# Hybrid GLA and convolution block: the mix projections as seven-product units, with the recurrent branch moved to the convolution's output projection

## The chip, the cores and the metric

The kernel runs on one core of one Trainium2 chip. The metric is the device time of one execution in microseconds (us), here the median over runs. Five engines work side by side, each through its own list of instructions in a fixed order: PE (TensorE, matmuls, with PEld for its weight loads), DVE (VectorE), ACT (ScalarE), POOL (GpSimd) and SP (SyncE, which here only issues transfers). They wait for each other by semaphores. POOL and ACT issue some of the transfers too.

## What is computed

A block of 1024 tokens plus 16 meta tokens in front (L = 1040; LQ = 1026 are kept), width 1024, in fp32:

```python
u = rms_norm(h, norm_mix_g)                 # h: meta tokens, then x
q, k, v, r, a_lr, c_in, g_gla, g_conf = split(u @ w_in)
o = gla_chunked(q, k, v, log_a(a_lr))       # gated linear attention, 4 heads, chunks of 64
o = rms_norm(o per head) * silu(r)
gla = o @ w_gla_o
c = c_in[:, :1024] * sigmoid(c_in[:, 1024:])
y = causal_dwconv(c, 31 taps) + bias        # each channel by itself
conv = silu(layer_norm(y)) @ w_conf_o
h = h + (sigmoid(g_gla) * gla + sigmoid(g_conf) * conv) @ w_out
h = h + gated ConvFFN(rms_norm(h))          # w_up, 3-tap convolution, silu gate, w_down
out = rms_norm(h) without the meta tokens
```

## The kernel before, in words

Activations lie channel by channel: a tile holds 128 channels by up to 1040 tokens. An fp32 matmul is emulated: every operand is split into a high part (float32r) and the rest, and `mm3` (L178) issues three matmuls for each of the 8 tiles of the inner dimension: high times high (L187), low times high (L188), high times low weights (L189). A block of 128 output channels is therefore 24 matmuls for each group of columns.

The program runs through these stages: the norm of x and three blocks by column chunks (alpha, q and k of head 0); 54 plain projection blocks (`block`, 72 matmuls of 342 to 348 columns each) for q, k, v, r, the two halves of c and the two gates; the GLA output projection (576 matmuls of 342 columns); the convolution's output projection (768 of 258 or 252); the projection w_out; the FFN's up projection; w_down.

The up projection already uses a seven-product scheme: two blocks of 128 outputs that share their inputs are a unit. The weights of both (raw tiles r1 and r2) are quartered and combined by four sums on POOL (L792 to L795), and the products of the combined weights with combined halves of the activations need 7 products of 24 matmuls in place of the 8 that two plain blocks would take for the same columns. `unit_weights` (L786) makes the weights w1, w21, w34 and w2 of a unit, `unit_products` (L823) issues the products and adds them up, and for the first four units `unit_head` issues two products ahead.

Plain weights are split in `load_w` (L171): a raw load on SP's queue, two copies on ACT (L173 makes the negated raw, L174 the high part), and a transfer from DRAM on POOL's queue that adds the raw values onto the first (L175), which leaves the low part. Tiles come from pools: three raw weight tiles, three split pairs, 35 slots of activations. An instruction that writes a tile waits until the readers of the tile's last user are done.

Beside the projections two generators are fed piece by piece by `tick()`, which every column group of a block calls. `conv` (L365) is the 31-tap convolution of one channel tile, one DVE instruction per tap (L367, then L370 on the whole tile, each on the result of the last), at 2.2 pieces a tick; POOL adds its result to `ysum` (L377). `gla` (L390) is one head of the recurrent branch, at 1.35 pieces a tick: decay factors from POOL, ACT and DVE at several band widths (L442 to L446), small matmuls on them (L457, L476), then the states chunk by chunk (L537 to L549) and the norm (L566). `layer_norm` (L612) runs beside the last gates. q, k, v and c go from PSUM into SBUF slots and are read there. A scheduler writes each engine's order from these calls, their priorities and dependences.

## Time and profile before

| what | value |
|---|---|
| median of 2 runs | 1843.58 us (1843.4 to 1843.75) |
| the profiled execution | 1847.21 us |
| its span in the trace | 1845.4 us |
| mean granted TensorE clock | 0.983 |
| PE busy | 1776.2 us, 96% |
| DVE, ACT, POOL busy | 1156.4, 705.6, 444.8 us |

The chain that ended last consists of PE to 80% and of DVE to 13%. A stage is read by its stretch: the plain projections with GLA and convolution beside them run from 64 to about 824 us, the GLA output projection to 915, the convolution's to 1007, w_out to 1101, the up projection to 1571, w_down to the end. In a stretch where PE is busy all the time, the number of matmuls and the length of one set the time; where it is not, another engine or a transfer does.

### The profile page before, as it was taken

How to read it: one execution, taken by the hardware profiler on the slowest of the kernel's cores; microseconds unless marked ns; L12 is line 12 of the kernel's file. 1: busy time of each engine (PE TensorE's matmuls, PEld its weight loads, DVE VectorE, ACT ScalarE, POOL GpSimd, SP SyncE). 2: the span in 40 equal slices, each digit the busy share in tenths (PEclk: the TensorE clock that was granted, in tenths of full speed). 3: DMA queues.
4: the chain of work that ended last, by engine and by line, in shares of the span. 5: the costliest groups of instructions: out<-in, count | busy, mean ns of one | idle time of the engine just before them, and what ended most of it. 6: DMA issues, size and time to landing. Idle time of an engine off the chain costs nothing.

```text
span 1845.4 us, 28931 instructions
## 1 busy us (share of the span) xinstructions
PE 1776.2 (96%) x12210; PEld 1692.7 (92%) x12210; DVE 1156.4 (63%) x1350; ACT 705.6 (38%) x1050; POOL 444.8 (24%) x333
## 2 busy tenths in 40 slices
PE   4999999999999999999999997999999999899997
PEld 3999999999999999999999997999999999677886
DVE  5239976968878860733455369877667666733523
ACT  5325436426435743691222333222222223423321
POOL 2103223313413412200000256333333334200000
PEclk7999999999999999999999998999999999999999
DMA  6343335324334544453133441222221224634532
GB/s 211 79 92 87 65 80 125 70 71 114 69 80 103 121 124 120 153 192 137 35 137 129 164 132 35 100 73 77 86 79 69 87 86 151 207 116 154 158 119 66
DMA packets 63442, 200.93 MB, mean 109 GB/s; under 512 B 6864, under 2 KB 14160, under 8 KB 63312
## 3 DMA queue, kind: packets, MB, share of 16 engines
q1 hardware_dynamic: 51168, 159.03, 26.4%
q0 software_dynamic: 10368, 37.75, 10.2%
q10 hardware_dynamic: 1776, 2.30, 0.4%
q8 instruction: 96, 1.57, 0.4%
q14 instruction: 34, 0.28, 0.0%
HBM read 162.31 MB, written 36.74 MB: 108 GB/s over the span
## 4 chain that ended last, share of the span: by engine, by line
PE 80%; DVE 13%; DMA 2%; issue 2%; ACT 2%; POOL 1%; SPq 0%; DVEq 0%; ACTq 0%; POOLq 0%
PE mm L187 13%; PE mm L188 13%; PE mm L189 13%; PE prod L187 12%; PE prod L189 12%; PE prod L188 12%; DVE y L370 5%; DVE opl L228 1%; DVE wl L162 1%; PE g L476 1%; DVE E L445 1%; DMA x<-in_xT 1%; PE g L544 1%; PE g L537 1%; PE g L545 1%
## 5 line engine op out<-in xcount | busy, mean ns | idle before, releaser
L187 PE MATMUL mm<-uh,wh 128*128 128x342 f32 (+4 forms) x1344 | 445.7, 332 | 0.0
L188 PE MATMUL mm<-ul,wh 128*128 128x342 f32 (+4 forms) x1344 | 435.0, 324 | 0.0
L189 PE MATMUL mm<-uh,wl 128*128 128x342 f32 (+4 forms) x1344 | 433.0, 322 | 0.0
L188 PE MATMUL prod<-opl,wh 128*128 128x258 f32 x1232 | 349.7, 284 | 12.1 <-DVE opl L228 11.8
L187 PE MATMUL prod<-oph,wh 128*128 128x258 f32 x1232 | 350.1, 284 | 4.8 <-DVE t L832 4.8
L189 PE MATMUL prod<-oph,wl 128*128 128x258 f32 x1232 | 350.4, 284 | 0.0
L370 DVE SCALAR_TENSOR_TENSOR y<-c,pv,y 128x1026 f32<-128x1026 f32 x240 | 342.3, 1426 | 5.4
L161 ACT ACTIVATE wh<-wr 128x1024 fp32r<-128x1024 f32 (+2 forms) x152 | 147.7, 974 | 382.5 <-PE prod L188 175.2
L162 DVE TENSOR_TENSOR wl<-wr,wh 128x1024 fp32r<-128x1024 f32 (+2 forms) x134 | 159.0, 1189 | 175.6 <-ACT wh L161 174.3
L187 PEld LDWEIGHTS mm<-uh,wh 128*128 128x128 f32 x1344 | 255.7, 190 | 5.4 <-issue 3.7
L188 PEld LDWEIGHTS mm<-ul,wh 128*128 128x128 f32 x1344 | 255.5, 190 | 1.7 <-issue 0.6
L189 PEld LDWEIGHTS mm<-uh,wl 128*128 128x128 f32 x1344 | 255.6, 190 | 0.7 <-issue 0.6
L188 PEld LDWEIGHTS prod<-opl,wh 128*128 128x128 f32 x1232 | 234.4, 190 | 13.3 <-DVE opl L228 12.7
L187 PEld LDWEIGHTS prod<-oph,wh 128*128 128x128 f32 x1232 | 234.4, 190 | 5.8 <-issue 3.2
L189 PEld LDWEIGHTS prod<-oph,wl 128*128 128x128 f32 x1232 | 233.9, 190 | 0.0
L189 PE MATMUL mm<-oph,wl 128*128 128x512 f32 (+1 forms) x374 | 143.6, 384 | 3.2 <-DVE wl L162 3.2
L187 PE MATMUL mm<-oph,wh 128*128 128x512 f32 (+1 forms) x374 | 143.9, 385 | 2.1 <-ACT wh L161 1.3
L188 PE MATMUL mm<-opl,wh 128*128 128x512 f32 (+1 forms) x374 | 144.6, 387 | 0.6 <-DVE opl L228 0.6
L187 PE MATMUL prod<-sh,wh 128*128 128x342 f32 (+2 forms) x448 | 133.8, 299 | 0.5 <-ACT gate L656 0.5
L175 POOL DMA_DIRECT2D wl<-in_w_mix x50 | 44.0, 880 | 372.2 <-ACT wl L173 318.3
L189 PE MATMUL prod<-sh,wl 128*128 128x342 f32 (+2 forms) x448 | 133.4, 298 | 0.0
L188 PE MATMUL prod<-sl,wh 128*128 128x342 f32 (+2 forms) x448 | 133.4, 298 | 0.0
(239 smaller groups left out, 2852.4 us busy)
## 6 DMA issues: line engine op xcount, KB each, us to landing
wr<-in_w_mix SPq DMA_DIRECT2D x56, 512.0 KB, 3.9
wl<-in_w_mix POOLq DMA_DIRECT2D x50, 512.0 KB, 8.1
wr<-in_w_up SPq DMA_DIRECT2D x48, 512.0 KB, 3.3
wr<-in_w_o SPq DMA_DIRECT2D x32, 512.0 KB, 3.5
wr<-in_w_dn SPq DMA_DIRECT2D x32, 512.0 KB, 3.6
act_d<-fy SPq DMA_DIRECT2D x21, 512.0 KB, 2.6
ar<-act_d POOLq DMA_DIRECT2D x21, 512.0 KB, 6.6
wr<-in_w_dn SPq DMA_DIRECT2D x16, 384.0 KB, 3.2
```

The costliest lines, as they stand in the source:

```text
L161: pin(S.activation(hi, raw, AF.Copy))
L162: (eng or V).tensor_tensor(lo, raw, hi.bitcast(F32), op=ALU.subtract)
L175: nc.gpsimd.dma_start(lo, src, accum_op=ALU.add)
L187: PE.matmul(out, whi[:, wk], hi[:, c0:c1], start=first and k == 0, stop=False)
L188: PE.matmul(out, whi[:, wk], lo[:, c0:c1], start=False, stop=False)
L189: PE.matmul(out, wlo[:, wk], hi[:, c0:c1], start=False, stop=last and k == n - 1)
L228: (eng or V).tensor_tensor(lo, src, hi.bitcast(F32), op=ALU.subtract)
L370: V.scalar_tensor_tensor(y[:, :LQ], c[:, j : j + LQ], pcol("dw_w", i * CONV_K + j), y[:, :LQ], op0=ALU.mult, op1=ALU.add)
L445: V.tensor_tensor(Ev[:, :, 0:s], Ev[:, :, 0:s], kv[:, :, 0:s], op=ALU.mult)
L476: PE.matmul(pt[:, c * half : (c + 1) * half].rearrange("p (b t) -> p b t", t=s), lt[:, sl], right(rt[:, sl], s), start=True, stop=True)
L537: PE.matmul(kv_ps[:, :DVH], kdT[:, c * CH : (c + 1) * CH], vc(c), start=True, stop=True)
L544: PE.matmul(op[:, :DVH], qd[:, c * CH : (c + 1) * CH], sts[c], start=True, stop=False)
```

## The change

The 54 plain blocks become 27 units of seven products (168 matmuls of 260 columns each), in this order: 8 units of c alternating with 8 of gates, 3 of q and k (heads 1 to 3), 4 of v, 4 of r. `unit_products` takes a new form for all units but the first four, here and in the FFN: partial results stay in two PSUM banks (`chain`, `twin`) onto which further products accumulate, and ACT copies the intermediate sums. The results of every unit go to DRAM (`done`), and their readers load them again. The weights of the new units are made with `by_dma`: the low parts of w1, w34 and w2 come from adding transfers on POOL's queue, of w34 with the combined tile in SBUF as its source, and POOL itself subtracts for w21. There are four split pairs in place of three, 34 slots of 1040 columns in place of 35 of 1056, and x and u lie in pairs of channel tiles per half of 520 tokens.

The convolution runs beside the units (1.9 pieces per product), reading c back from DRAM, its sum `ysum` is added up by a transfer, and the layer norm is queued behind it. After all units, GLA runs (5.8 pieces a tick, a second head may start while the first is in its states) beside the convolution's output projection, which now precedes the GLA output projection. Cut to its core, the diff is:

```diff
     wraw = ctx.enter_context(tc.tile_pool(name="wraw", bufs=3))
-    wspl = ctx.enter_context(tc.tile_pool(name="wspl", bufs=3))
+    wspl = ctx.enter_context(tc.tile_pool(name="wspl", bufs=4))
...
+    def split_from(src, raw):
+        hi, lo = weight_pair(raw.shape[-1])
+        pin(S.activation(lo, raw, AF.Copy, scale=-1.0))
+        pin(S.activation(hi, raw, AF.Copy))
+        nc.gpsimd.dma_start(lo, src, accum_op=ALU.add)
+        return hi, lo
...
+    active = []
...
+        if q is gla_q:
+            if not active:
+                active.append(q.popleft())
+            done = next(active[0], None)
+            if done is None:
+                active.pop(0)
+            else:
+                active.append(active.pop(0))
+                if done == 2 and q:
+                    active.append(q.popleft())
...
+    def conv(i):
+        c = slot(nm="c")
+        nc.sync.dma_start(c[:, :L], c_d[i])
+        taps = [META] + [j for j in range(CONV_K) if j != META]
+        for j in taps:
+            o = max(META - j, 0)
+            src, dst, wcol = c[:, j + o - META : j - META + LQ], y[:, o:LQ], pcol("dw_w", i * CONV_K + j)
+            if j == META:
+                V.tensor_scalar(dst, src, wcol, pcol("dw_b", i), op0=ALU.mult, op1=ALU.add)
+            else:
+                V.scalar_tensor_tensor(dst, src, wcol, dst, op0=ALU.mult, op1=ALU.add)
             yield 1
...
+        nc.gpsimd.dma_start(ysum_d, y[:, :LQ], **({"accum_op": ALU.add} if i else {}))
...
+        sr = [reload(sr_d[2 * h + d], "sr") for d in range(2)]
+        yield 2
...
+            PO.tensor_tensor(og[:, :LQ], og[:, :LQ], sr[d][:, :LQ], op=ALU.mult)
+            nc.sync.dma_start(og_d[2 * h + d], og[:, :LQ])
...
+    def unit_weights(src1, src2, ahead, full, by_dma):
+        with tc.high_priority(offset=ahead):
+            r1, r2 = load_raw(src1), load_raw(src2)
+            w1 = None
+            if full:
+                w1 = split_from(src1, r1) if by_dma else split_w(r1)
+            a11, a12, a21, a22 = r1[:, :512], r1[:, 512:], r2[:, :512], r2[:, 512:]
+            s1, s2 = Pt[:, 512:], Pt[:, :512]
+            PO.tensor_tensor(s1, a21, a22, op=ALU.add)
+            PO.tensor_tensor(s2, s1, a11, op=ALU.subtract)
+            PO.tensor_tensor(a11, a11, a21, op=ALU.subtract)
+            PO.tensor_tensor(a12, a12, s2, op=ALU.subtract)
+            if by_dma:
+                w21 = split_w(Pt, PO)
+                w34 = split_from(r1, r1)
+                return w1, w21, w34, split_from(src2[:, 512:], a22)
+            if full:
+                w21, w34 = split_w(Pt), split_w(r1, PO)
+            else:
+                w34, w21 = split_w(r1), split_w(Pt)
+            return w1, w21, w34, split_w(a22)
+
+    def product(w, c0, op, h, onto=None, more=False):
+        pt = bank("prod") if onto is None else onto
+        whi, wlo = w
+        for q in range(2):
+            out = pt[:, q * 512 : q * 512 + h // 2]
+            for k in range(4):
+                hi, lo = op[k // 2]
+                a0 = (k % 2) * h + q * h // 2
+                wk = slice(c0 + k * P, c0 + (k + 1) * P)
+                for x, y, n in ((whi, hi, 0), (whi, lo, 1), (wlo, hi, 2)):
+                    PE.matmul(out, x[:, wk], y[:, a0 : a0 + h // 2], start=onto is None and k == n == 0,
+                              stop=k == 3 and n == 2, skip_group_check=more or onto is not None)
+        tick()
+        return pt
+    def unit_head(w1, ops, h):
+        sums, halves = unit_parts(h)
+        a = slot(nm="fa")
+        p1 = halves(a[:, h:])
+        S.activation(p1, sums(product(w1, 0, ops["B11"], h)), AF.Copy)
+        V.tensor_tensor(halves(a), sums(product(w1, 512, ops["B21"], h)), p1, op=ALU.add)
+        return p1, a
...
+        chain = product(w1, 0, ops["B11"], h, more=True)
+        S.activation(a1, sums(chain), AF.Copy)
+        V.tensor_tensor(a0, sums(product(w1, 512, ops["B21"], h)), a1, op=ALU.add)
+        product(w21, 0, ops[2], h, chain, more=True)
+        S.activation(a1, sums(chain), AF.Copy)
+        twin = product(w21, 512, ops[1], h, more=True)
+        S.activation(b1, sums(twin), AF.Copy)
+        product(w34, 0, ops[3], h, chain)
+        S.activation(b0, sums(chain), AF.Copy)
+        V.tensor_tensor(b1, b1, b0, op=ALU.add)
+        product(w34, 512, ops["B22"], h, twin)
+        V.tensor_tensor(a1, sums(twin), a1, op=ALU.add)
...
+    C, GATE, QK, VAL, R = range(5)
+    units = [u for i in range(8) for u in ((C, i, NB_C2 + i, NB_C1 + i), (GATE, i, NB_G + i, NB_H + i))]
+    units += [(QK, h, NB_Q + h, NB_K + h) for h in range(1, HEADS)]
+    units += [(VAL, h, NB_V + 2 * h, NB_V + 2 * h + 1) for h in range(HEADS)]
+    units += [(R, h, NB_R + 2 * h, NB_R + 2 * h + 1) for h in range(HEADS)]
...
+            S.activation(a[:, :L], a[:, :L], AF.Sigmoid)
+            V.tensor_tensor(b[:, :L], b[:, :L], a[:, :L], op=ALU.mult)
+            nc.sync.dma_start(c_d[i], b[:, :L])
+            conv_q.append(conv(i))
+            if i == KT - 1:
+                conv_q.append(layer_norm())
...
+    heads = [unit_head(load_w(w_mix[units[f][2]], True), ops, HA) for f in range(HEADS_A)]
+    ws = [weights_a(0)]
+    differences(xs, ops, HA)
+    ws.append(weights_a(1))
+    rate["conv"] = 1.9
+    for f, (kind, i, _, _) in enumerate(units):
+        if 0 < f < len(units) - 1:
+            ws.append(weights_a(f + 1))
+        done(kind, i, *unit_products(ws.pop(0), heads.pop(0) if heads else None, ops, HA))
     drain(conv_q)
-    ln_q.append(layer_norm())
+    V.memset(Pt, 0.0)
+    open_banks(mm=(4, 512), g=(4, 512))
+    prefetch(2)
+    cfp = [operand(reload(ys_d[i], "ys"), LQ) for i in range(KT)]
+    gla_q.extend(gla(h) for h in range(HEADS))
+    rate["gla"] = 5.8
...
+        gc = reload(gc_d[i], "gc")
+        block(next_w(), cfp, CHUNKS_Q if i == KT - 1 else CHUNKS_H, 0,
+              lambda pt, c0, n: V.tensor_tensor(gc[:, c0 : c0 + n], pt, gc[:, c0 : c0 + n], op=ALU.mult),
+              ogp_first if i == KT - 1 else None)
+        nc.sync.dma_start(br_d[i], gc[:, :LQ])
...
```

Two places show how the engines' lists move. First POOL, in the middle of the projections, from head 1's accumulating weight loads (`wl<-in_w_mix`) over the sum of convolution results (`ysum`) to the norm of GLA (`rst`), before:

```order
L443 TENSOR_TENSOR E_4385<-nb_3811 128x256x2
L446 TENSOR_TENSOR E_4385<-E_4385,q_2456 128x256x2
L175 DMA wl_4601<-in_w_mix 128x1024
L383 MEMSET c_4596 128x16
L175 DMA wl_4733<-in_w_mix 128x1024
L377 TENSOR_TENSOR ysum_603<-ysum_603,y_4136 128x1026
L175 DMA wl_4901<-in_w_mix 128x1024
L175 DMA wl_4997<-in_w_mix 128x1024
L566 TENSOR_TENSOR rst_4850<-rst_4850,nhalf 128x9
```

and after the change, one unit and a half (`Pt` and `wr` are the combined and raw weights, `wl` the low parts of w1, w21, w34 and w2 in this order, w34's with the raw tile `wr_4034` as source):

```order
L408 DMA ysum_d_468<-y_3575 128x1026
L176 DMA wl_3831<-in_w_mix 128x512
L660 TENSOR_TENSOR Pt<-wr_4036 128x512
L661 TENSOR_TENSOR Pt<-Pt,wr_4034 128x512
L176 DMA wl_4039<-in_w_mix 128x1024
L662 TENSOR_TENSOR wr_4034<-wr_4034,wr_4036 128x512
L663 TENSOR_TENSOR wr_4034<-wr_4034,Pt 128x512
L169 TENSOR_TENSOR wl_4048<-Pt,wh_4047 128x1024
L176 DMA wl_4052<-wr_4034 128x1024
L176 DMA wl_4057<-in_w_mix 128x512
```

The decay factors are gone from this stretch. In their place stand four sums, a subtraction and three adding transfers for each unit, and w1's transfer comes behind the first two sums, which read the raw tile of the second block.

Second PE, where a head of GLA builds its levels (`g<-E`, from the decay factors of 64, 32, 16 and more columns), before; `mm` are matmuls of a plain projection block:

```order
L188 MATMUL mm_1463<-ul_119,wh_1284 128x346
L189 MATMUL mm_1463<-uh_118,wl_1285 128x346
L187 MATMUL mm_1463<-uh_120,wh_1284 128x346
L188 MATMUL mm_1463<-ul_121,wh_1284 128x346
L189 MATMUL mm_1463<-uh_120,wl_1285 128x346
L457 MATMUL g_1489<-E_1393 64x64 x8
L187 MATMUL mm_1501<-uh_106,wh_1284 128x346
L188 MATMUL mm_1501<-ul_107,wh_1284 128x346
L189 MATMUL mm_1501<-uh_106,wl_1285 128x346
L187 MATMUL mm_1501<-uh_108,wh_1284 128x346
L188 MATMUL mm_1501<-ul_109,wh_1284 128x346
L189 MATMUL mm_1501<-uh_108,wl_1285 128x346
```

and after, beside the convolution's output projection:

```order
L519 MATMUL g_7232<-q_7099,km_7198 15x1
L520 MATMUL g_7232<-ident,km_7198 16x128
L481 MATMUL g_7240<-E_7207 64x64 x8
L194 MATMUL mm_7694<-opl_7062,wh_7019 128x252
L195 MATMUL mm_7694<-oph_7061,wl_7020 128x252
L193 MATMUL mm_7694<-oph_7067,wh_7019 128x252
L194 MATMUL mm_7694<-opl_7068,wh_7019 128x252
L195 MATMUL mm_7694<-oph_7067,wl_7020 128x252
L481 MATMUL g_7282<-E_7226 32x32 x16
L533 MATMUL g_7301<-vmeta_7137,kmT_7238 128x256
L481 MATMUL g_7313<-E_7276 16x16 x32
L500 MATMUL g_7356<-E_7307 128x64 x8
```

Before, 24 matmuls of a block follow on each level of a head; now five stand between the first two levels and none behind them up to the block after the last level.

## Rows read from the trace of the kernel before

**Rows 1.** The page's first section, busy time and share by engine.

```profile
PE 1776.2 (96%) x12210; PEld 1692.7 (92%) x12210; DVE 1156.4 (63%) x1350; ACT 705.6 (38%) x1050; POOL 444.8 (24%) x333
```

**Rows 2.** Stretches: us; busy of PE, PEld, DVE, ACT, POOL; clock; DMA share; GB/s.

```profile
0.00:64.00 64.00, 40.90 (x169) 32.09 (x170) 38.43 (x78) 31.98 (x63) 17.08 (x22) 0.81 0.50 152
64.00:148.00 84.00, 84.00 (x524) 84.00 (x523) 28.87 (x30) 27.89 (x41) 7.15 (x10) 1.00 0.46 104
...
266.00:413.00 147.00, 144.53 (x1000) 139.57 (x1000) 116.73 (x130) 68.20 (x115) 41.19 (x34) 0.99 0.37 87
...
704.00:824.00 120.00, 118.95 (x741) 115.75 (x739) 49.62 (x55) 76.83 (x98) 18.18 (x11) 1.00 0.51 162
824.00:915.00 91.00, 90.46 (x580) 90.46 (x581) 32.78 (x57) 21.02 (x41) 0.00 (x0) 1.00 0.30 100
915.00:1007.00 92.00, 92.00 (x769) 92.00 (x768) 55.30 (x119) 25.31 (x51) 0.00 (x0) 1.00 0.31 108
...
1130.00:1170.00 40.00, 31.24 (x215) 29.94 (x215) 37.32 (x28) 11.06 (x12) 23.70 (x11) 0.83 0.13 41
...
1190.00:1545.00 355.00, 354.12 (x2945) 353.85 (x2945) 250.29 (x250) 93.82 (x105) 133.92 (x89) 1.00 0.23 79
```

**Rows 3.** Groups by line: busy us, mean ns of one, idle before, releasers.

```profile
L370 DVE SCALAR_TENSOR_TENSOR y<-c,pv,y 128x1026 f32<-128x1026 f32 x240 | 342.3, 1426 | 5.4
...
L174 ACT ACTIVATE wh<-wr 128x1024 fp32r<-128x1024 f32 x50 | 52.8, 1056 | 150.9 <-PE mm L188 125.8 <-issue 22.7 <-PE mm L184 2.3
...
L175 POOL DMA_DIRECT2D wl<-in_w_mix x50 | 44.0, 880 | 372.2 <-ACT wl L173 318.3 <-ACT t L562 44.7 <-DVE km L425 9.3
L162 POOL TENSOR_TENSOR wl<-wr,wh 128x1024 fp32r<-128x1024 f32 x18 | 43.0, 2386 | 84.5 <-ACT wh L161 84.5
L446 POOL TENSOR_TENSOR E<-E,q 128x512 f32<-128x512 f32 x24 | 42.2, 1769 | 74.3 <-ACT E L444 74.3
L443 POOL TENSOR_TENSOR E<-nb 128x512 f32<-128x512 f32 x24 | 34.2, 1515 | 0.3 <-DVE km L425 0.3
...
L793 POOL TENSOR_TENSOR Pt<-Pt,wr 128x512 f32<-128x512 f32 x22 | 32.4, 1471 | 1.7
L795 POOL TENSOR_TENSOR wr<-wr,Pt 128x512 f32<-128x512 f32 x22 | 31.0, 1408 | 0.0
...
L794 POOL TENSOR_TENSOR wr<-wr,wr 128x512 f32<-128x512 f32 x22 | 30.0, 1364 | 78.0 <-DVE wl L162 77.7
L792 POOL TENSOR_TENSOR Pt<-wr 128x512 f32<-128x512 f32 x22 | 29.2, 1327 | 92.9 <-DMA wr<-in_w_up 59.2 <-DVE fy L855 17.4 <-DVE fa L845 11.0
...
L377 POOL TENSOR_TENSOR ysum<-ysum,y 128x1026 f32<-128x1026 f32 x7 | 16.7, 2387 | 18.6 <-DVE y L370 18.6
...
L842 DVE TENSOR_TENSOR t<-prod,t 128x516 f32<-128x516 f32 x22 | 15.3, 696 | 22.9 <-PE prod L189 22.7
...
L566 POOL TENSOR_TENSOR rst<-rst,nhalf 128x9 f32<-128x9 f32 x4 | 10.2, 2556 | 0.3 <-DVE rst L565 0.3
...
L836 ACT ACTIVATE t<-prod 128x516 f32<-128x516 f32 x17 | 9.9, 585 | 2.0 <-PE prod L189 2.0
```

**Rows 4.** Transfers by issuer: count, KB each, median us from issue to landing.

```profile
wr<-in_w_mix SPq DMA_DIRECT2D x56, 512.0 KB, 3.9
wl<-in_w_mix POOLq DMA_DIRECT2D x50, 512.0 KB, 8.1
```

**Rows 5.** The accumulating transfers of L175 between 300 and 420 us.

```profile
DMA to landing us min/median/max: 6.3/7.8/8.9
```

**Rows 6.** Timeline from 149 us, three taps: start, length, what.

```profile
149.03 3.94 DVE L370 SCALAR_TENSOR_TENSOR y<-c,pv,y 128x1026 f32<-128x1026 f32 x3
```

**Rows 7.** Timeline from 1407 us: a DVE line without and with POOL beside it.

```profile
1407.08 1.28 DVE L852 SCALAR_TENSOR_TENSOR fy<-fa,pv,fy 128x1024 f32<-128x1024 f32 x1
...
1408.44 2.38 POOL L162 TENSOR_TENSOR wl<-wr,wh 128x1024 fp32r<-128x1024 f32 x1 [4.80 <-ACT wh L161]
...
1408.88 3.04 DVE L852 SCALAR_TENSOR_TENSOR fy<-fa,pv,fy 128x1024 f32<-128x1024 f32 x1
```

More of the change, by code (lines that the diff above doesn't have):

```diff
@@ L35 @@
 LN_EPS = 1e-5
-SLOT = 1056
-CHUNKS_S = [(0, 256), (256, 392), (648, 392)]
+NSLOT = 34
+SLOT = 1040
+HA = 520
+QA = HA // 2
+CHUNKS_A = [(i * QA, QA) for i in range(4)]
 CHUNKS_L = [(0, 348), (348, 346), (694, 346)]
@@ L182, in mm3 @@
             for k, (wk, (hi, lo)) in enumerate(pairs):
-                PE.matmul(out, whi[:, wk], hi[:, c0:c1], start=k == 0, stop=False)
-                PE.matmul(out, whi[:, wk], lo[:, c0:c1], start=False, stop=k == n - 1)
+                PE.matmul(out, whi[:, wk], hi[:, c0:c1], start=first and k == 0, stop=False)
+                PE.matmul(out, whi[:, wk], lo[:, c0:c1], start=False, stop=last and k == n - 1)
             return
@@ new lines, in differences, with minus, made @@
+    def differences(un, ops, h):
+        w = slice(0, 2 * h)
+        def minus(eng, out, x, y):
+            eng.tensor_tensor(out[:, w], x[:, w], y[:, w], op=ALU.subtract)
+        def made(name, x, y, eng=None):
+            ops[name] = [operand(x, 2 * h), operand(y, 2 * h, eng)]
+        (p0, p1, q0, q1), (r0, r1, t0, t1) = un
+        minus(V, p0, r0, p0)
+        if "B22" not in ops:
+            ops["B22"] = [operand(t0, 2 * h)]
+        minus(V, p1, r1, p1)
+        if len(ops["B22"]) < 2:
+            ops["B22"].append(operand(t1, 2 * h))
+        minus(PO, r0, t0, r0)
+        made(1, p0, p1)
+        minus(PO, r1, t1, r1)
+        minus(V, p0, t0, p0)
+        minus(V, p1, t1, p1)
+        made(3, r0, r1, PO)
+        made(2, p0, p1, PO)
+        minus(V, q0, q0, p0)
+        minus(V, q1, q1, p1)
+        made(4, q0, q1, PO)
```

388 lines of the change are left out of this document (151 added, 237 removed).

## The prediction, made before the changed kernel was run

> **What bounds the kernel now.** I read the busy times first [rows 1]: PE works 96% of the span, DVE 63%, POOL 24%. A table by stretches [rows 2] says what kind of work that is. From 64 to 148 us 524 matmuls of 346 to 348 columns fill PE, 84.00 / 524 = 160 ns each. From 824 to 915 us 580 of 342 columns take 90.46 us, 156 ns each. From 915 to 1007 us 769 of 258 or 252 columns take 92.00 us, 119.6 ns each, and in the FFN, 1190 to 1545 us, 2945 of 258 columns take 354.12 us, 120.2 ns. The time follows the columns at full clock. So in the projections the number of columns sets the end, and fewer products are worth their full length, as long as PE stays the engine that is waited for. In the same stretches the reader is to see how full the others are: in one head of the old projections (266 to 413 us) DVE is busy for 116.73 of 147 us and POOL for 41.19. In the FFN, where seven-product units already run, PE idles under 1 us of 355. Half of the question is thus whether the new units have room for the convolution beside them; the other half is where GLA goes.
>
> What GLA costs PE now: the stretch of one head holds 10 blocks of 72 matmuls at 158 ns, 113.8 us, so 33 us of its 147 are not projections. Four heads make 134 us.
>
> **What it removes.** 54 blocks of 72 matmuls, half at 156 and half at 160 ns: 1944 × 0.156 + 1944 × 0.160 = 614 us. In their place stand 27 × 168 = 4536 matmuls of 260 columns; by the rows of 258 columns, 120.6 ns: 547 us, 20.3 us a unit. **-67 us**, if PE never waits.
>
> **The units beside the convolution.** From the fifth unit on DVE has, per unit, the taps: 8 × 31 with the first on each tile, of which some 222 fall into 18 units, 12.3 a unit. A tap that follows another takes 3.94 / 3 = 1.31 us where POOL is quiet [rows 6], the mean is 1.426 [rows 3]. That is 16.1 us. Three evacuations from PSUM at 0.69 us [rows 3], a sum in SBUF that I price the same, and half a gate product: 3.2. Together 19.3 us of 20.3, before POOL disturbs. POOL has four sums (1.327, 1.471, 1.364, 1.408) and a subtraction of 2.386 us per unit [rows 3], 7.96 us. What that does to a DVE instruction stands in the timeline [rows 7]: the same line takes 1.28 us alone and 3.04 where a 2.38 us subtraction on POOL overlaps it. The price of POOL's 7.96 us lies between 1.7 (the mean of a tap over a lone one, 12.3 × 0.12 and a little) and 6.3 (all of POOL's time that falls on DVE's 80% of SBUF work). Line L852 as a whole loses 0.74 us per instruction where it meets such work, about half of the overlap, so I take the middle, 4. DVE needs 23.3 us per unit: 3.0 more than PE, over 18 units **+54 us** (ends 21.0 and 25.6: +13 and +95).
>
> The Trainium skill ("SBUF — State Buffer", section "SBUF: two separate sides") states that VectorE and GpSimd share one port pair as an exclusive lock, held for the whole instruction by whichever starts first. The trace agrees at one place, since 1.28 + 1.76 = 3.04 us, and by that rule alone a unit would take the upper end, 25.6 us.
>
> The weights give a second bound on a unit. Only four split pairs exist, so the four of the next unit come free one by one: w1's place after product 4 of the unit before, w34's only at its end. Their making is a chain: raw load 3.9 us [rows 4], sums L660 and L661 2.8 us, two ACT copies at 1.06 [rows 3], an adding transfer. The raw tile is released only when w34's transfer has read it, and w1's transfer stands behind the two sums on POOL's queue, as the order shows. Followed over two units this closes: 2T = one unit's products 20.3 + copies 2.1 + transfer A + load 3.9 + sums 2.8 + transfer A, about 29.1 + 2A. The adding transfers from DRAM land after 8.1 us in the median [rows 4], and after 6.3 to 8.9 in one head [rows 5]; no row shows one whose source is in SBUF. With A = 8.1, T = 22.6; with 6.3, 20.9; it would be hidden from 5.7 on. So beside the convolution DVE decides by a little, and in the five units after it the weights do: 5 × 2.1 = **+10 us** (0 to 16).
>
> **The first four units.** They have two products ahead, five are left, 14.5 us of PE. Each needs one round on POOL: w34's transfer 7.8, the raw load 3.9, sums 5.6, subtraction 2.4, about 19.9 us. The first unit's weights are made under the products ahead, three rounds are not covered: 3 × 5.4 = **+16 us** (0 to 22).
>
> **GLA beside the convolution's output projection.** PE's own work there is 92 [rows 2] + 134 = 226 us. But the second place of the order shows that five matmuls, 0.6 us, separate the first levels of a head and nothing the later ones, where 24 of 160 ns stood before. A level needs 1.515 + 1.769 = 3.3 us of POOL [rows 3], so five levels after the first make PE wait up to 16.4 us; on the same queue stand the norm (2.56 us) and two products of the head before, which I price as the sum of line L377, 2.39 each [rows 3]. Between 0 and 66 us for four heads, I take a third, **+23 us**, since POOL starts on a head while PE still has projections from the block before and the states of the head ahead. ACT's and DVE's work there has room.
>
> **Small ones.** The norm in four chunks instead of three, in a stretch where PE works 40.90 of 64 us [rows 2]: **+3**. After such waits the granted clock falls: 0.83 over the 40 us from 1130 to 1170 us, where PE worked 31.24 us [rows 2], worth (1 - 0.83) × 40 = 7 us; two or three such places, not all of them long: **+5** (0 to 20). The layer norm leaves the gates, where 760 - 614 - 134 = 12 us are neither blocks nor GLA, and comes to stand among the last units with its reloads on SP's queue ahead of raw weights: 0. The new form of the units moves three sums of 0.69 us from DVE to ACT copies of 0.585 in the FFN [rows 3], where PE has no gap to win back: 0, or at worst 0.5 us for 17 units. GLA output projection, w_out and w_down keep their matmuls: 0. The convolution's results, q, k, v and gates pass DRAM under the units, at a DMA share of 0.4 to 0.5 now: 0, and if they collide, it shows in A.
>
> **The sum.** -67 + 54 + 10 + 16 + 23 + 3 + 5 = +44 us. The profiled execution took 1847.2 us with a span of 1845.4; the median of the runs is 1843.6, and I add to that: **1888 us**. A change within 2% (37 us, 1807 to 1880) counts as the same, which is about what a measurement of this kernel can tell.
>
> **Rivals.**
> First, POOL shuts DVE out for all of each overlap: units of 25.6 us, +41 on the sum, and DVE's part of GLA loses about 20 more next to POOL's products. 1949 us. For it speaks the row of 3.04 us, against it the mean tap of 1.426, which was measured beside POOL's work of the old heads. Chance 0.20.
> Second, both bounds are milder: adding transfers of 6.3 us and little contention, T = 21 us, 0.8 × 18 + 0.6 × 5 = 17 instead of 64 us, and 10 instead of 23 us in GLA: 1888 - 47 - 13 = 1828 us. Chance 0.20.
> Third, the other side: PE stays the bound, as it does in the FFN today, whose units make the same sums on POOL. It decides if w34's transfer from SBUF lands within 5.7 us and a tap costs no more than (20.3 - 3.2) / 12.3 = 1.39 us, so that DVE fits into 20.3 us; then the two terms of +64 vanish, and with GLA's levels covered, -67 + 16 + 3 + 5 = -43: 1801 us, or 1785 if the first four units are hidden as well. For it speaks the FFN's 99.8%; against it, DVE has 250.29 / 355 × 20.2 = 14.2 us of work per unit there and 19.3 here. Chance 0.14.
> That the products are not saved I leave out: the order shows 168 rows per unit.
>
> **The numbers.** The forecast itself, 1860 to 1920 us, has 0.46, and the likeliest place is 1888. The range is 1805 to 1945: below it lies most of the third rival, above it the upper half of the first. Faster by over 2% are the third rival and a little of the second, 0.16; within 2% most of the second and the lower part of the forecast, 0.36; slower 0.48.
>
> **What would show it.** Product tiles of the fifth to the 22nd unit should start 23.3 us apart, with PE's idle time ended by DVE's PSUM sums or by the transfers into `wl`; in the last units 22.4 with weights as the releaser. A lone tap stays at 1.3 and the mean goes to 1.6 to 1.7. The stretch of the convolution's output projection should last about 250 us, PE's idle time there ended by POOL's factors. If the units start every 20.3 us, the third rival is right; if the adding transfer from SBUF lands in under 5 us, the weights' chain falls; and if the stretch with GLA is near 226 us, POOL's levels were covered.

## The result: 14% slower, and the profile after

The changed kernel takes 2107.3 us (median of 2 runs, 2102.05 to 2112.55) where the one before takes 1843.58: a ratio of 1.143, 95% interval 1.131 to 1.155. The forecast had the direction right (1888 us, slower) and the size far too small; the time lies 162 us above the end of the range. The profiled execution took 2112.55 us with a span of 2110.6.

The first section of the page, as in [rows 1]:

```profile
PE 1813.2 (86%) x13092; PEld 1712.4 (81%) x13092; DVE 1336.3 (63%) x1426; ACT 774.8 (37%) x1142; POOL 729.6 (35%) x488
```

PE is busy for 37 us more than before, although it has 67 us less of products to do. The stretches tell where; columns as in [rows 2], the cuts at the stages: norm and first blocks, first four units, units 5 to 22 beside the convolution, the last five units with the layer norm, the convolution's output projection with GLA, the GLA output projection, w_out, the FFN's up projection, w_down.

```profile
0.00:77.00 77.00, 49.69 (x289) 42.84 (x290) 49.35 (x103) 41.69 (x94) 24.92 (x31) 0.96 0.53 155
77.00:196.00 119.00, 91.93 (x672) 89.86 (x672) 71.73 (x59) 40.17 (x45) 61.86 (x39) 0.89 0.48 124
196.00:680.00 484.00, 396.13 (x3027) 389.87 (x3027) 433.37 (x309) 173.74 (x221) 228.59 (x153) 0.92 0.59 146
680.00:853.00 173.00, 121.56 (x850) 117.09 (x850) 60.82 (x60) 72.37 (x88) 41.94 (x34) 0.83 0.75 208
853.00:1176.00 323.00, 256.92 (x1864) 229.25 (x1864) 174.84 (x300) 145.55 (x295) 102.52 (x63) 0.82 0.40 123
1176.00:1270.00 94.00, 93.75 (x770) 93.78 (x771) 53.04 (x110) 22.69 (x43) 0.00 (x0) 0.98 0.41 145
1270.00:1365.00 95.00, 93.00 (x772) 92.51 (x771) 50.25 (x70) 35.58 (x58) 37.20 (x28) 1.00 0.58 170
1365.00:1835.00 470.00, 452.09 (x3703) 449.25 (x3701) 322.68 (x289) 166.11 (x205) 210.73 (x120) 0.99 0.24 86
1835.00:2110.60 275.60, 258.13 (x1152) 207.96 (x1152) 120.27 (x130) 76.93 (x97) 21.83 (x21) 0.97 0.41 134
```

From 1176 us on all is as it was: 934.6 us, where the kernel before needs 930.4 from 915 us to its end (one of the two output projections and all that follows). In particular the new form of the units does nothing to the FFN, 470 us in both. The whole loss lies ahead of that: 1176 us in place of 915. The granted clock stands at 0.82 to 0.92 in the four stretches from 77 to 1176 us, where PE has gaps; most of PE's extra busy time lies there. The largest misses are the units (484 and 173 us) and the stretch with GLA (323 us).

Beside the convolution, between 230 and 440 us, the same table gives

```profile
230.00:440.00 210.00, 175.24 (x1352) 172.25 (x1351) 200.88 (x141) 78.84 (x100) 101.12 (x67) 0.93 0.58 144
```

DVE is busy 96% of it, PE 83%. 1352 matmuls are 8.05 units, 26.1 us each. The groups by line between 210 and 680 us (busy us, mean ns, idle before, as in [rows 3]) show why DVE is full:

```profile
L405 DVE SCALAR_TENSOR_TENSOR y<-c,pv,y 128x1026 f32<-128x1026 f32 (+8 forms) x212 | 342.0, 1614 | 5.1
...
L169 POOL TENSOR_TENSOR wl<-Pt,wh 128x1024 fp32r<-128x1024 f32 x18 | 54.0, 2998 | 3.0 <-ACT wh L168 3.0
...
L663 POOL TENSOR_TENSOR wr<-wr,Pt 128x512 f32<-128x512 f32 x18 | 35.8, 1988 | 0.0
L661 POOL TENSOR_TENSOR Pt<-Pt,wr 128x512 f32<-128x512 f32 x17 | 34.7, 2041 | 1.3
...
L662 POOL TENSOR_TENSOR wr<-wr,wr 128x512 f32<-128x512 f32 x18 | 30.4, 1689 | 0.0
L734 DVE TENSOR_TENSOR fb<-fb 128x520 f32<-128x520 f32 x18 | 29.6, 1644 | 1.9 <-ACT fb L733 1.9
L660 POOL TENSOR_TENSOR Pt<-wr 128x512 f32<-128x512 f32 x17 | 28.4, 1671 | 114.1 <-DMA wr<-in_w_mix 114.1
...
L736 DVE TENSOR_TENSOR fa<-prod,fa 128x520 f32<-128x520 f32 x18 | 12.4, 688 | 1.5 <-PE prod L684 1.5
```

A tap takes 1.614 us on average, where it took 1.31 alone [rows 6] and 1.426 on average before [rows 3]. Over the whole run the median tap takes 1.286 us and the longest 6.276: most are as short as alone, and those that meet POOL's work pay. L734 is a sum of 520 columns with both operands in SBUF: 1.644 us. L736 is a sum of as many columns with one operand in PSUM: 0.688 us, as before (0.696 for L842 [rows 3]). POOL's sums too are longer than the 1.33 to 1.47 us of [rows 3]. One place of the timeline of DVE, and of POOL beside it (start, length), shows it on one tap:

```profile
485.58 1.75 DVE L734 TENSOR_TENSOR fb<-fb 128x520 f32<-128x520 f32 x1
487.26 3.37 DVE L405 SCALAR_TENSOR_TENSOR y<-c,pv,y 128x1015 f32<-128x1015 f32 x1
490.55 0.69 DVE L736 TENSOR_TENSOR fa<-prod,fa 128x520 f32<-128x520 f32 x1
```

```profile
484.55 2.22 POOL L663 TENSOR_TENSOR wr<-wr,Pt 128x512 f32<-128x512 f32 x1
486.74 2.81 POOL L169 TENSOR_TENSOR wl<-Pt,wh 128x1024 fp32r<-128x1024 f32 x1
```

The tap that starts at 487.26 lasts 3.37 us; POOL's subtraction (`wl<-Pt,wh`) ends at 489.55, and the tap 1.08 us later.

### The profile page after: what moved, and what is told of

It reads as the page before. It is cut to its first block, busy times and chain, and to the rows that moved or that the text cites. A ratio compares the mean times of both kernels' runs of the same rounds, so it can differ in the third digit from the quotient of the medians.

```text
span 2110.6 us, 31630 instructions
## 1 busy us (share of the span) xinstructions
PE 1813.2 (86%) x13092; PEld 1712.4 (81%) x13092; DVE 1336.3 (63%) x1426; ACT 774.8 (37%) x1142; POOL 729.6 (35%) x488
## 3 DMA queue, kind: packets, MB, share of 16 engines
q8 instruction: 102, 1.67, 0.3%
## 4 chain that ended last, share of the span: by engine, by line
PE 43%; DVE 6%; issue 5%; DMA 4%; ACT 3%; POOL 3%; DVEq 0%; SPq 0%; POOLq 0%; ACTq 0%
PE prod L684 20%; PE mm L193 4%; PE mm L194 4%; PE mm L195 4%; PE prod L193 3%; PE prod L194 3%; PE prod L195 3%; PE g L500 2%; DMA yr<-y_d 1%; DMA br_d<-gc 1%; POOL E L470 1%; POOL E L467 1%; DVE wl L169 1%; DVE opl L237 1%; DMA ys<-ys_d 1%
## 5 line engine op out<-in xcount | busy, mean ns | idle before, releaser
L684 PE MATMUL prod<-oph,wh 128*128 128x258 f32 (+1 forms) x2096 | 606.8, 290 | 49.9 <-ACT fa L726 26.4
L684 PE MATMUL prod<-opl,wh 128*128 128x258 f32 (+1 forms) x2096 | 604.0, 288 | 18.4 <-POOL opl L237 9.8
L684 PE MATMUL prod<-oph,wl 128*128 128x258 f32 (+1 forms) x2096 | 603.4, 288 | 13.7 <-DMA wl<-in_w_mix 8.7
L684 PEld LDWEIGHTS prod<-opl,wh 128*128 128x128 f32 x2096 | 407.3, 194 | 20.3 <-POOL opl L237 10.4
L405 DVE SCALAR_TENSOR_TENSOR y<-c,pv,y 128x1026 f32<-128x1026 f32 (+8 forms) x240 | 388.3, 1618 | 5.3
L684 PE MATMUL prod<-uh,wl 128*128 128x260 f32 x648 | 198.4, 306 | 72.5 <-DMA wl<-in_w_mix 65.4
L193 PE MATMUL mm<-oph,wh 128*128 128x512 f32 (+4 forms) x622 | 220.4, 360 | 10.2 <-ACT oph L236 6.3
L195 PE MATMUL mm<-oph,wl 128*128 128x512 f32 (+4 forms) x622 | 222.1, 358 | 4.0 <-DVE wl L169 4.0
L194 PE MATMUL mm<-opl,wh 128*128 128x512 f32 (+4 forms) x622 | 224.0, 361 | 1.1 <-DVE opl L237 1.1
L684 PE MATMUL prod<-uh,wh 128*128 128x260 f32 x648 | 196.1, 303 | 25.1 <-ACT fb L731 19.9
L684 PE MATMUL prod<-ul,wh 128*128 128x260 f32 x648 | 195.1, 301 | 0.0
L684 PEld LDWEIGHTS prod<-uh,wh 128*128 128x128 f32 x648 | 135.6, 209 | 26.3 <-ACT fb L731 20.5
```

The source lines that it names most:

```text
L193: PE.matmul(out, whi[:, wk], hi[:, c0:c1], start=first and k == 0, stop=False)
L194: PE.matmul(out, whi[:, wk], lo[:, c0:c1], start=False, stop=False)
L195: PE.matmul(out, wlo[:, wk], hi[:, c0:c1], start=False, stop=last and k == n - 1)
L405: V.scalar_tensor_tensor(dst, src, wcol, dst, op0=ALU.mult, op1=ALU.add)
L684: PE.matmul(out, x[:, wk], y[:, a0 : a0 + h // 2], start=onto is None and k == n == 0, stop=k == 3 and n == 2, skip_group_check=more or on ...
```

## Experiments

All were timed in three rounds beside the kernel before; the ratio is to that kernel, with its 95% interval. The change has two runs, 10.5 us apart, the others four each, so a difference of the medians under some 10 us decides nothing. A stage's own length repeats better. In ten runs whose units beside the convolution are untouched (the change, e4, e6 to e8, e10, e11, e13 to e15) a unit takes 26.7 to 27.2 us; in six whose stretch with GLA is untouched (the change, e1, e2, e3, e5, e9) it is 323 to 327 us from the start of the units' last matmul to the first one of the GLA output projection. The lengths of single stretches in the table are cut as in the result. e3, e5, e8, e10 and e13 leave out a part of the computation. Line numbers move by a few where an edit adds lines.

| run | median us | ratio | what changed in the trace |
|---|---|---|---|
| the change | 2107.3 | 1.143 [1.131, 1.155] | |
| e1_swap | 2115.9 | 1.146 [1.142, 1.149] | nothing, 27.2 us a unit |
| e2_late | 2105.8 | 1.142 [1.139, 1.144] | 26.2 us a unit, the layer norm's units longer |
| e3_notaps | 2021.3 | 1.095 [1.093, 1.097] | 22.1 us a unit between 230 and 440, the layer norm among later ones |
| e4_early | 2121.0 | 1.149 [1.146, 1.152] | stretch with GLA 335 us |
| e5_nopool | 2020.3 | 1.093 [1.091, 1.095] | 22.9 us a unit |
| e6_lnslow | 2114.5 | 1.145 [1.142, 1.147] | the layer norm's waits moved, not gone |
| e7_stagec | 2091.7 | 1.132 [1.130, 1.134] | stretch with GLA 298 us |
| e8_nogla | 1928.9 | 1.044 [1.042, 1.045] | stretch without GLA 138 us |
| e9_w21dma | 2087.2 | 1.131 [1.127, 1.134] | 25.5 us a unit |
| e10_noln | 2041.9 | 1.107 [1.104, 1.110] | last five units 107 us |
| e11_lnafter | 2077.4 | 1.125 [1.123, 1.128] | last units and norm 153 us |
| e12_best | 2036.2 | 1.103 [1.100, 1.105] | the gains of e7, e9 and e11 |
| e13_noproj | 2093.6 | 1.133 [1.131, 1.136] | stretch with GLA 299 us |
| e14_early2 | 2114.4 | 1.145 [1.143, 1.147] | stretch with GLA 318 us |
| e15_early2c | 2104.7 | 1.141 [1.139, 1.144] | stretch with GLA 315 us |

The mean of a unit is taken from the first sum of the fifth unit to that of the 23rd; in the kernel of the change it is 26.9 us.

**What holds the units: the weights' chain or DVE.** In the trace PE's waits there end with w1's transfer, ACT stands behind DVE's last sum of a unit, and SP's raw loads behind w34's transfer. That suggested a loop through the raw weight tiles.

e1_swap:

```diff
-            r1, r2 = load_raw(src1), load_raw(src2)
+            if by_dma:
+                r2, r1 = load_raw(src2), load_raw(src1)
+            else:
+                r1, r2 = load_raw(src1), load_raw(src2)
```

> In the new units the raw tile of the second block is loaded ahead of that of the first, so that the tile whose place the next load takes is the one that w2's copies release and not the one that w34's transfer reads. Theory A (raw tiles): a unit's period, 26.7 us on average between the fifth and the 22nd, is a closed loop of raw load, POOL sums, w34's copies on ACT, w34's transfer and the next raw load; the swap takes w34's transfer (5 us) out of it, and the period falls to DVE's 23 to 24: 18 x 3 = 50 us or more, 2040 to 2060 us. Theory B (DVE): the taps beside POOL set the period and the transfers only happen to come last: within 10 us of 2107.

e2_late:

```diff
-        done(kind, i, *unit_products(ws.pop(0), heads.pop(0) if heads else None, ops, HA))
+        late.append((kind, i, *unit_products(ws.pop(0), heads.pop(0) if heads else None, ops, HA)))
+        if len(late) > 1:
+            done(*late.pop(0))
```

> The work on a unit's results (sigmoid, silu, scale, stores, start of the convolution) is written one unit later, so that ACT does not wait in it for DVE's last sum of the unit. Theory A with ACT's queue as a link: in the trace ACT stood 4 to 8 us behind DVE's sum ahead of w34's two copies; without that wait the loop is 3 to 5 us shorter, 50 to 80 us in all, 2030 to 2055 us. If the loop is made of transfers alone, or if DVE sets the period, nothing: 2095 to 2115 us.

Neither moved the time. What PE waited for between 230 and 440 us (us, times, longest), first in the changed kernel, then in e1_swap:

```profile
PE prod L684 <- DMA wl<-in_w_mix: 25.4, 7, 6.6
```

```profile
PE prod L687 <- ACT fa L729: 16.3, 5, 6.4
PE prod L687 <- ACT fb L734: 13.5, 7, 2.7
PE prod L687 <- DMA wl<-in_w_mix: 3.0, 1, 3.0
```

In e1_swap PE waits for copies on ACT instead, and a unit is as long as ever: the last releaser had changed, the bound had not. Theory A, as the bound at 26 us, falls.

e3_notaps:

```diff
-        taps = [META] + [j for j in range(CONV_K) if j != META]
+        taps = [META]
```

> 30 of the 31 taps are left out (the convolution keeps its reload, one tap, its store and its sum). Theory A: POOL and ACT are no longer held by DVE, but the loop of raw load 5, sums 4, difference and split, copies 2, transfer 5 and its issue stays: a unit still takes 20.5 to 22 us, with waits for w1's transfer left in some, about 2010 us. Theory B: the units run at PE's 20.3 us and no wait for weights is left, 1985 us. Both gain; the trace tells them apart by what PE waits for.

e5_nopool:

```diff
+            w = slice(0, 8 if by_dma else 512)
-            PO.tensor_tensor(s1, a21, a22, op=ALU.add)
+            PO.tensor_tensor(s1[:, w], a21[:, w], a22[:, w], op=ALU.add)
...
-                w21 = split_w(Pt, PO)
+                w21 = weight_pair(1024)
+                pin(S.activation(w21[0], Pt, AF.Copy))
+                pin(S.activation(w21[1], Pt, AF.Copy, scale=-1.0))
```

> In the new units POOL's four sums run on 8 columns in place of 512, and w21's low part is a copy on ACT in place of POOL's subtraction: the weights are left uncombined, all else stays, the 31 taps too. Theory B (DVE is the bound of the units, and POOL's 8 us a unit lengthen its taps): between 230 and 440 us DVE was busy 200.9 of 210 us, 25.1 a unit, where its work alone needs 19.3; without POOL's work the units fall from 26.4 to 20.5 to 21.5 us and the mean tap from 1.6 to 1.3: 18 x 5 = 90 us, 2005 to 2025 us. Rival (DVE's taps are too many even alone, or the transfers hold the units): 24 to 25 us a unit, 2070 us.

The stretch from 230 to 440 us, first of e3_notaps, then of e5_nopool:

```profile
230.00:440.00 210.00, 198.50 (x1598) 197.48 (x1597) 51.61 (x48) 96.48 (x121) 101.80 (x82) 0.97 0.71 175
```

```profile
230.00:440.00 210.00, 196.29 (x1570) 195.06 (x1569) 174.68 (x160) 100.29 (x126) 54.39 (x69) 0.96 0.70 172
```

Without the taps it holds 9.51 units, 22.1 us each, and PE still waits 11.5 us for w1's transfer: that is what theory A expected of e3_notaps, and theory B's 20.3 us without a wait is missed. With all taps but little work on POOL (its four sums take 3.2 us a unit, where sums and subtraction took 10.4) it holds 9.35, 22.5 us each, and DVE is at 83%, 18.7 us a unit. The groups of e5_nopool between 210 and 680 us (L737 is the sum that was L734):

```profile
L405 DVE SCALAR_TENSOR_TENSOR y<-c,pv,y 128x1026 f32<-128x1026 f32 (+8 forms) x204 | 261.3, 1281 | 5.0
...
L737 DVE TENSOR_TENSOR fb<-fb 128x520 f32<-128x520 f32 x19 | 13.3, 698 | 19.4 <-ACT fb L736 19.4
```

A tap is back at 1.281 us and the sum in SBUF at 0.698, from 1.614 and 1.644. So the taps are long because POOL works beside them, and the units are long because both meet: without either they fall to 22 us. e5_nopool took 87 us off the whole, 71 of them in the 18 units (22.9 in place of 26.9 us) and 17 ahead of the fifth unit's first sum. It also takes POOL's sums out of the making of the weights; that the taps and not these sums carry the loss rests on DVE's 96% and on e1_swap. The units do not reach PE's 20.3 us, nor the 20.5 to 21.5 expected; what PE waits for then is w1's transfer, 13.7 us in these 210, so the weights come next, close to the 22.4 us that the forecast gave them.

e9_w21dma takes one of POOL's five instructions away and leaves the result whole:

```diff
-                w21 = split_w(Pt, PO)
+                w21 = split_from(Pt, Pt)
```

> w21's low part comes from an adding transfer with the combined tile in SBUF as its source, as w34's does, in place of POOL's subtraction (3.0 us beside the taps). POOL's work falls from 10.4 to 7.4 us a unit. Theory B with the contention as its cause: what the taps lose to POOL (5.8 us a unit) falls in that proportion, to 4.1, and the 18 units beside the convolution get 1.7 us shorter each: 30 us, 2070 to 2085 us. Rival: the combined tile is held until the transfer has read it, so the next unit's first sum waits some 5 us more and the weights set the unit: 2105 us or more.

20 us less; units of 25.5 us in place of 26.9, and again 25.5 in e12_best, which has the same edit; a mean tap of 1.471 in place of 1.618 over all 240. So a part of POOL's work gives back a part of the loss, if less than the 30 us expected; the rival is out.

**What the layer norm costs among the last units.** The chain of waits of the changed kernel from 737 us on, in order of time:

```profile
737.10 5.33 DMA yr<-y_d
...
742.46 1.24 DVE yr L626
...
743.72 5.33 DMA y_d<-yr
...
749.15 1.07 ACT yr L628
...
750.24 1.24 DVE s L630
...
751.50 3.57 DMA yr<-y_d
...
755.09 1.24 DVE yr L626
...
756.35 3.56 DMA y_d<-yr
...
762.37 3.79 PE prod L637 x6
```

Each tile is reloaded (3.6 to 5.3 us), reduced, stored again and squared, one after the other, 10.8 to 14.4 us a tile here. DVE and ACT stand in their order behind it, with the units' sums and copies queued after. Two of the waits between 690 and 853 us show both ends of that, ACT's for the store and PE's for a copy of a unit:

```profile
ACT yr L628 <- DMA y_d<-yr: 25.2, 6, 11.1
```

```profile
PE prod L684 <- ACT fb L731: 17.0, 2, 16.2
```

e10_noln leaves `layer_norm` out:

> The layer norm is left out; the output projection reads the convolution's result. Theory: the last five units, 173 us, would take 23 us each without it, 115 us; 55 us less, 2045 to 2060 us. Rival (they are slow by their weights and stores, the DMA share is 0.76 there): 2085 us or more.

The last five units of e10_noln:

```profile
680.00:787.00 107.00, 103.58 (x836) 102.96 (x835) 22.01 (x24) 49.98 (x63) 42.24 (x34) 0.97 0.66 164
```

107 us for 836 matmuls, 21.5 us a unit, in place of 173: the norm costs 66 us there, and the theory holds. It also shows that without DVE's load the weights' chain costs these units at most 1.2 us each. e3_notaps has the norm among earlier units, and there two unit periods take 59.6 and 54.8 us in place of 22: some 70 us again.

e6_lnslow:

```diff
+        if len(conv_q) == 1 and f > 16:
+            rate["conv"] = 0.8
```

> Once the convolution is done, the layer norm is fed at 0.8 pieces a product in place of 1.9, over six units in place of three. Theory: the three units in which it stands took 35, 58 and 31 us in place of 26 because PE, ACT and SP wait in their order for its reloads and sums; spread out, these waits fall under products: 30 to 45 us less, 2062 to 2077 us. Rival (each piece costs its wait wherever it stands): 2100 us.

The time came out as the rival had it: from the first sum of the 23rd unit to the end of the norm it is 170 us in place of 165. But the theory was not put to its test, since the norm did not end under the products. Its last stretches (columns as in [rows 2]):

```profile
690.00:830.00 140.00, 110.04 (x807) 107.14 (x805) 48.28 (x55) 66.97 (x83) 42.32 (x33) 0.89 0.72 193
830.00:860.00 30.00, 0.00 (x0) 0.00 (x0) 6.14 (x5) 7.12 (x6) 0.55 (x1) 0.51 0.89 262
```

The units' last matmul starts 26 us earlier than in the changed kernel (823 in place of 849 us), and the rest of the norm then stands uncovered, 30 us without a matmul. e11_lnafter takes the norm out of the units, as a block after them with its tiles kept in SBUF:

```diff
-                conv_q.append(layer_norm())
...
+        ys = [reload(y_d[i], "yr") for i in range(KT)]
...
-    cfp = [operand(reload(ys_d[i], "ys"), LQ) for i in range(KT)]
+    cfp = [operand(y, LQ) for y in layer_norm()]
```

> The layer norm runs after the last unit, with its eight tiles loaded at once and kept in SBUF, in place of a reload, a store and again a reload and a store of each beside the units. Its own work then stands uncovered, about 8 x 1.24 + 8 x 1.24 + 8 x 1.24 us on DVE with small matmuls between, 38 us, but the reload of its results ahead of the output projection (20 us) goes. If the units' slots and queues are what the norm costs (theory), the units give back 55 us: 35 us less in all, 2065 to 2080 us; if the norm costs its work and no more, 15 us longer, 2120 us.

30 us less, within the range expected, though all of the norm's work is now uncovered: the units' last matmul starts 64 us earlier (785 us), and the stretch behind it is 28 us longer.

**What holds the stretch with GLA.** What PE waited for there in the changed kernel (us, times, longest):

```profile
PE g L500 <- POOL E L470: 13.8, 5, 5.1
PE prod L193 <- DVE gc L844: 13.2, 1, 13.2
PE g L605 <- DVE o L595: 7.6, 3, 3.0
PE g L519 <- ACT t L575: 6.3, 3, 2.4
PE mm L193 <- ACT oph L236: 6.3, 3, 3.7
```

e7_stagec:

```diff
+            eng = V if s in (32, 8, 2) else PO
+            eng.tensor_tensor(Ev[:, :, s : 2 * s], pv_[:, :, s : 2 * s], ref, op=ALU.subtract)
...
-            PO.tensor_tensor(og[:, :LQ], og[:, :LQ], sr[d][:, :LQ], op=ALU.mult)
+            V.tensor_tensor(og[:, :LQ], og[:, :LQ], sr[d][:, :LQ], op=ALU.mult)
```

> In GLA the factors of every second level (32, 8, 2) and the product of the output with silu(r) go from POOL to DVE. Theory C2 (POOL's queue is the link of a head's chain: six levels of 3.3 us and two products of 2.5): 27 us of POOL become 12 a head, DVE has 149 us idle in this stretch; the stretch of 323 us falls by 25 to 45, 2062 to 2082 us. Rival C3 (the chain goes through ACT, DVE and PE in turn and POOL is only one link): 0 to 10 us less.

The stretch fell by 25 us to 298, which is the least that C2 expected; the median fell by 16 (2107.3 to 2091.7), between both. POOL is a link of the chain, but not the whole.

e8_nogla:

```diff
     def gla(h):
+        sr = [reload(sr_d[2 * h + d], "sr") for d in range(2)]
+        yield 2
+        for d in range(2):
+            nc.sync.dma_start(og_d[2 * h + d], sr[d][:, :LQ])
+            yield 1
```

> GLA is left out: each head only passes silu(r) on as its output. What is left of the stretch is the convolution's output projection with its reloads, 92 us of matmuls, 10 ahead and 15 behind: about 120 us in place of 323, 1900 to 1910 us. GLA would then cost 200 us where it stands now, against 134 beside the plain projections. Rival (the stretch is long for its reloads and stores, not for GLA): over 150 us, 1935 us or more.

138 us are left, 27 of them a wait for a gate tile whose load stood behind the eight reloads that this kernel issues at once. That lies between the two expectations. By the stretches GLA costs 185 us in its new place, by the medians 178, and 212 if the wait of 27 us is counted as this kernel's own; in the old place it was 134 by the prediction's count.

e13_noproj:

```diff
-        block(next_w(), cfp, CHUNKS_Q if i == KT - 1 else CHUNKS_H, 0,
+        block(next_w(), cfp[:1], CHUNKS_Q if i == KT - 1 else CHUNKS_H, 0,
```

> In the convolution's output projection seven of the eight input tiles are left out, so PE has 12 us of it in place of 92; GLA, its loads and the gates stay. Theory C3 (the heads' own chain sets the stretch: log decay, factors, levels, in turn through ACT, DVE, POOL and PE, 63 us from head to head): the stretch of 323 us falls by less than half of the 80 us taken away, 285 to 305 us, 2070 to 2090 us. Theory C4 (PE's work plus waits that do not depend on it): by all of the 80 us, 240 to 250 us, 2030 us.

The stretch of e13_noproj:

```profile
857.00:1156.00 299.00, 185.98 (x1213) 153.23 (x1213) 167.11 (x289) 139.45 (x283) 98.44 (x63) 0.69 0.42 132
```

80 us of products are gone, and the stretch is 24 us shorter, the median 14: PE's work does not set it. From the first fine level of one head to that of the next it is 61 us on average, in the changed kernel 66. PE's busy time fell by 71 us, of 80, and its clock from 0.82 to 0.69. The fine levels (32 of 64 columns by 128) of the kernel before, the changed one and e13_noproj:

```profile
L476 PE MATMUL g<-E 128*128 128x64 f32 x192 | 24.3, 281 | 5.6 <-DVE E L445 5.6
```

```profile
L500 PE MATMUL g<-E 128*128 128x64 f32 x192 | 39.5, 394 | 14.5 <-POOL E L470 13.8 <-DVE E L469 0.6
```

```profile
L500 PE MATMUL g<-E 128*128 128x64 f32 x192 | 42.8, 421 | 15.4 <-POOL E L470 15.4
```

The same matmul takes 1.4 and 1.5 times as long as before, with PE emptier each time.

e4_early and e14_early2 prepare q, k and the log decay of the next head early:

```diff
+    def prepare(h):
+        if h < HEADS and h not in ready:
+            ready[h] = (reload(q_d[h], "q"), reload(k_d[h], "k"), log_alpha(h))
...
         x = level(8)
         yield 1
+        prepare(h + 1)
+        yield 1
```

> q, k and the log decay of the next head are prepared while the present head is at its levels, ahead of its start. Theory C1: beside the convolution's output projection a head's own chain (log decay 13 us, then factors, levels, fine levels) sets the 63 us from head to head, since the next head starts only after the levels of the one before; then the stretch of 323 us gets 30 to 45 us shorter, 2060 to 2075 us. Theory C2: POOL's factors and PE's order set it: 0 to 10 us.

> As e4_early, with the low-rank decay input kept in SBUF through the stretch: in e4_early PE waited 16.8 us for its reload, which hid what was to be seen. Theory C3: q, k and the log decay of the next head (13 us of its chain) are ready early for three heads: 20 to 40 us less, 2065 to 2085 us. Rival: the next head's work then stands in the queues ahead of the present one's and delays it: 2100 us or more.

Both miss: 2121.0 and 2114.4 us. In e14_early2 the second head's log decay starts at 909 us in place of 930, yet its first fine level at 973 as in the changed kernel, and the third's and fourth's at 1040 and 1108 as there: the log decay is not a link, and the early work delayed nothing either. e15_early2c adds e7's edit to it:

> e14_early2 together with e7_stagec (half of the factors and the output product on DVE; 16 us less by itself in the median). Theory C3 with POOL as one link: the two gains add, 2045 to 2070 us. If e14_early2 alone gives nothing, this gives what e7_stagec gave: 2085 to 2095 us.

It misses both values: 2104.7 us, and a stretch of 315 us where e7_stagec alone had 298. That the early work now stands in the queues ahead of the present head's, as the rival of e14_early2 had it, is the likely reason; it is not shown.

**All gains together.** e12_best is e7, e9 and e11 in one kernel.

> The three edits that leave the result whole, together: factors and output product half on DVE (25 us less when measured alone), w21 by a transfer, the layer norm after the units. If their places are independent, as theory B and the reading by stages have it, the gains add up: 25 + 30 + 35 = 90 us, 2005 to 2030 us; still slower than the kernel before by 160 us. If one bound lies behind all three, less than 50 us in all.

71 us less than the change, where the three alone gave 16, 20 and 30, 66 together: by the medians the places are independent. The 2005 to 2030 us expected are missed by 6, since 30 and 35 of the 90 us were the forecasts of e9 and e11 and not what they gave. It is still 10.3% slower than the kernel before. No version that computes everything beat that.

## Why the prediction was wrong, point by point

| term, us | forecast | measured | difference |
|---|---|---|---|
| norm and first blocks | 67 | 77 | +10 |
| first four units | 97 | 119 | +22 |
| units 5 to 22 | 419 | 484 | +65 |
| last five units, with the layer norm | 112 + 12 | 173 | +49 |
| convolution's output projection with GLA | 249 | 323 | +74 |
| clock after waits | 5 | in the rows above | -5 |
| from the GLA output projection on | 930 | 935 | +4 |

The forecasts are the prediction's (97 is 4 × 20.3 + 16, 249 is 226 + 23). The differences make 219 us, the whole miss. Two small sums of the prediction are off: 7.8 + 3.9 + 5.6 + 2.4 is 19.7 us and not 19.9, and a third of 66 is 22 and not 23; neither moves the forecast by 2 us.

**Units beside the convolution: the right bound, mis-sized.** The step that DVE sets them at 19.3 us plus what POOL takes held; that I took the middle of the contention, 4 us of 1.7 to 6.3, failed. My grounds were that line L852 loses half of an overlap; measured, it is the upper end: 26.1 us a unit between 230 and 440, 25.6 by the first rival. DVE was busy 25.0 us a unit, 5.7 more than its own 19.3 and 6.3 more than in e5_nopool. The mean tap of the kernel before hid it: POOL was busy for 41 of 147 us beside those taps [rows 2], and for 101 of 210 beside the new ones. The first rival had this price, at a chance of 0.20; e5_nopool and e9_w21dma show it as the cause.

The Trainium skill's rule in the prediction ("SBUF — State Buffer", section "SBUF: two separate sides") counts to the lock a VectorE instruction with two inputs in SBUF. The trace agrees, with 1.644 us against 0.698 for the sum in SBUF beside POOL's work and with little of it, and 0.688 beside it for the sum that reads PSUM. The prediction's 1.28 + 1.76 = 3.04 us tests nothing, since 1.76 is only the difference. What can be compared is the time left: 1.94 us of POOL's subtraction were left when that instruction started [rows 7] and it lost 1.76; 2.29 us were left for the tap at 487.26, and it lost 2.1.

**The weights' chain: right as the next bound, not as the one of the last units.** The adding transfers of w1 and w34 took 5.4 and 5.5 us (issue to landing, median), not 6.3 to 8.1; w2's, of half the size, which the chain leaves out, 6.9:

```profile
wr<-in_w_mix SPq DMA_DIRECT2D x60, 512.0 KB, 5.4
...
wl<-in_w_mix POOLq DMA_DIRECT2D x29, 512.0 KB, 5.4
wl<-wr POOLq DMA_DIRECT2D x27, 512.0 KB, 5.5
...
wl<-in_w_mix POOLq DMA_DIRECT2D x27, 256.0 KB, 6.9
```

The one whose source is in SBUF is no slower than the one from DRAM. By this alone the chain would be hidden, at the forecast's own break-even of 5.7. But a raw load takes 5.4 us in place of 3.9 [rows 4], and beside the taps the two sums 3.7 in place of 2.8; with these the forecast's sum gives 2T = 20.3 + 2.1 + 5.4 + 3.7 + 5.4 + 5.5, T = 21.2 us. The units without taps or without POOL's sums take 22.1 and 22.5, and the last units of e10_noln 21.5, 6 us more than PE's 20.3 for the five: the +10 us were a few us too large, made of a transfer priced too long and a load priced too short, and the layer norm hid them.

**The layer norm: nothing added for its new place, 66 us in place of 12.** I moved its 12 us along and looked at its work; I named its reloads on SP's queue and gave them no price. A reload and a store per step, in the order of engines that also serve the units, are a chain of 10.8 to 14.4 us a tile. Of the +49 of this row it makes 54, and the units without it -5 (107 in place of 112).

**The stretch with GLA: the wrong bound.** I took PE's 226 us, added a third of POOL's levels, and gave ACT and DVE room there. e13_noproj shows that PE's work is nearly free there: with 80 us less of it a head still takes 61 us. What I missed is that a step through POOL, ACT, DVE and PE is then paid with hardly any independent work behind it in PE's list, level after level; before, 24 matmuls of a projection or more followed on each. That this is why no order tried here covers the chain is argued from the lists, not shown. Half of the factors and the output product off POOL give 25 us of the stretch (e7_stagec). Which other links make up a head's time stays open: the log decay is not one (e14_early2).

**The first four units.** POOL's round was seen as the bound; the stretch came out 22 us longer than forecast. POOL's sums and subtraction take 9.4 us a unit there in place of 7.96, and in e5_nopool, with little of that work, the fifth unit's first sum comes 17 us earlier. The rest of this row, and the 10 us of the **front**, were not taken apart.

**The third rival** (PE stays the bound) needed a tap below 1.39 us and w34's transfer below 5.7. The second came true and the first did not.

**The clock.** 5 us was far too little: PE's busy time rose by 37 us with 67 us less to do, so PE spends about 104 us more on its matmuls than the forecast's rows at full clock, most of it where the granted clock was 0.82 to 0.92, and partly inside waits that would have been there anyway. It follows each gap of the other terms.

## What to carry to other kernels

A row of "mean" time for an instruction holds for the company that it had; before adding work to POOL beside a DVE that is nearly full, look for the one place where both run, and price the whole overlap. What ends a wait last is not what sets the period: one edit moved the transfer that ended PE's waits and one the work that ACT stood in, and nothing changed, while taking work off the busiest engine, or from beside it, did. And work that is to hide a chain of short steps over several engines (here one head of GLA) has to stand between the steps in the in-order lists; this last is how I read the lists, and no run here shows it.
